# RWKV stage of a hybrid decoder step: ScalarE without transfers, one root per group-norm row, the chain's y through a dead tile, later pooling and key transposition

## The chip, the core and the metric

The kernel runs on one core of a Trainium2 chip. TensorE (PE in the profile) does the matrix products, VectorE (DVE) and ScalarE (ACT) the work on rows, GpSimd (POOL) some small copies, and SyncE (SP) issues most of the transfers (DMA). Each engine executes its own instructions strictly in their order and waits at an instruction until the semaphores that it names have come. The metric is the device time of one execution in microseconds.

## The reference, cut to what matters

One layer of a decoder trunk, over 1024 prompt tokens and 8 requests of 8 tokens each, 1088 columns in all; D_MODEL is 1024, with 8 heads of 64.

```python
P = h @ w_in                       # h: RMSNorm and adaLN of x
pr, pp, pg = jnp.split(P, ...)     # RWKV columns, pooling columns, gates
o_r = rwkv7_branch(pr)             # state S per head, updated token by token:
#   sa = -S kk;  S = S * w + sa (kk a)^T + v k^T;  y = S r
#   y = (y - mean(y)) * rsqrt(var(y) + GN_EPS) * ln_w + ln_b   per head
#   y = (y + bonus) * g,  g = sigmoid(xg) @ g2
o_p = pool_branch(pp)              # means over 2/4/8/16 tokens, minus the token, @ pool_w
merged = sigmoid(g_r) * (o_r @ w_br_rwkv) + sigmoid(g_p) * (o_p @ w_br_pool)
x = x + gt * (merged @ w_out)
x = x + gt2 * (square(relu(h2 @ w_ff1)) @ w_ff2)
y = rms_norm(x, norm_final)
```

The outputs are y, the new token-shift and pooling buffers and the new RWKV states, for the prompt and for the requests.

## The kernel before

Features lie on the 128 partitions and tokens along the row, so a row is 128 x 1088. Each big product is done three times in a one-pass format, with weights and inputs cut into a rounded half (hi) and the rest (lo): hi hi, hi lo, lo hi. A row is cut into the column blocks CH of 364, 362 and 362. A job is one output block of 128 features: it loads its weights (`weights`, L391: a transfer on SP, hi on ScalarE, lo on VectorE or, for every second one from the 68th on, on POOL), multiplies over all input blocks into three PSUM banks named mm, and evicts them.

The first stage (`phase1`, L1401) interleaves two streams on TensorE. The **background** is a list of jobs: 14 for the RWKV columns (`rwkv_cols`), four for pooling (`pool_cols`), each followed by two gate jobs, then eight more gate jobs (`gate`), then eight branch jobs for the pooling branch (`op_job`, L1474). The second gate job of a pooling group is held until that group's pooling is done. The row tiles px (two of them) and d are shared in turn by all of these; an `op_job` loads its gate row th into one of them when it begins, uses it in the eviction at its end, and stores it from there. The **foreground** is a set of generators: `heads`, `chains`, `pools` and `or_rows`. One head row f (0 to 3) holds two heads. For each, `front` makes the decay, keys and queries; `scores` runs `unit` three times (prompt half 0, the samples, prompt half 1); `inverse`, `level` and `affine` invert the triangular system of every 64-token block and turn it into block-wise state updates; `sample` does the requests; `post` is group norm, bonus and output gate. `chain` carries the state S from block to block, 8 steps in each half, and gives y in a PSUM bank named wc. `post` of row f - 1 runs beside `inverse`, `level` and `affine` of row f; for the last row it comes at the end, in pieces (`piece`). After this stage the second stage (`phase2`) starts with jobs that multiply all four rows of `post`.

**What sets the order.** TensorE's order is written out by a planner in the program (`Pace.run`, L272): it keeps a time, adds an estimate for each product, and asks the foreground generators in their order whether their next step is due; if none is, it emits one background step of three products. A step says when it is due by `need` (L378): the planner's estimate of when its operands are ready plus `spare` (300 ns by default), and of when the PSUM banks it takes are free (`Need.at`, L220). `Clocks` (L79) keeps these estimates, with a cost for each instruction. The planner decides the order alone; on the chip TensorE then waits where an operand is late. The other engines' orders and the slots of the tiles are chosen by the framework's scheduler from a simulation, not by the program. Foreground products use the PSUM banks named w (two), and for the chain wc (two).

The places that the change touches:

- `pools` (L774): per group and column block, `need(z, plw, zs, wait=0)` and a product with `pool_w`.
- `unit` (L909): after the decays are multiplied into the tile bk, values and r/a rows are transposed on TensorE (evicted to uv by ScalarE, to at by VectorE), then the keys bk four blocks at a time (`tr`, the products at L389), evicted to ab.
- `chain` (L1119): y of each half leaves its bank in two copies of 256 columns on ScalarE, through one buffer of its own, each stored by SP; the state goes out at the end.
- `sample` (L1161): loads the requests' state s0 into one of three hv tiles and stores the new one from it.
- `post` (L1217): five tiles named wt are shared by all rows of this part. `rinv` (L561) is a root on ScalarE and a reciprocal on VectorE, per column block. `gate` loads g2, then bv (the bonus), then sg (sigmoid of xg), multiplies g2 with sg and leaves the product in sg. `self.wt(over)` tells the planner which tile's place the new one is thought to take.

Of the kernel before, what the change touches and what calls it, by code (L numbers as in the profile page):

```python
# [9 lines left out]
F32 = mybir.dt.float32  # L10
# [8 lines left out]
P = 128  # L19
# [59 lines left out]
class Clocks:  # L79
# [5 lines left out]
    def __init__(self, pace):  # L85
        self.pace, self.on = pace, False
        self.busy = {"vector": [], "scalar": [], "gpsimd": [], "sync": []}
        self.seen, self.slots, self.table = {}, {}, 0
# [125 lines left out]
class Need:  # L214


    def __init__(self, k, aps, banks, wait, spare):
        self.k, self.aps, self.banks, self.wait, self.spare = k, aps, banks, wait, spare

    def at(self):  # L220
        return max([self.k.clocks.ready(*self.aps) + self.spare] + [self.k.clocks.free(b, self.k.pb[b], self.banks.count(b)) for b in set(self.banks)])

    def __call__(self):
        return self.at() <= self.k.pace.t
# [97 lines left out]
class K:  # L322
# [52 lines left out]
    def room(self, ns=1000, eng="vector"):  # L375
        return Room(self, eng, ns)

    def need(self, *aps, banks=("w",), wait=1000, spare=300):  # L378
        return Need(self, aps, banks, wait, spare)

    def tr(self, out, in_, ident):
        if self.mode != (P, P):
# [178 lines left out]
    def rinv(self, ps, n, out, scale, eps):  # L561
        nc = self.nc
        nc.scalar.activation(out, ps[:, :n], AF.Sqrt, bias=self.eps[:, eps:eps + 1], scale=scale)
        for a in range(0, n, 182):
            nc.vector.reciprocal(out[:, a:min(a + 182, n)], out[:, a:min(a + 182, n)])

# [141 lines left out]
    def gate(self, b, dst):  # L708
        nc = self.nc
        S = {}  # L710

        def begin():
            th = S["th"] = self.px()
            return lambda c0, n, ps: nc.scalar.activation(th[:, c0:c0 + n], ps[:, :n], AF.Tanh, scale=0.5)

        return Job(self.w_in(b), begin, after=lambda: nc.sync.dma_start(dst, S["th"][:, :NT]), xs=self.hx_rows)
# [57 lines left out]
    def pools(self):  # L774

        nc = self.nc
        self.pl = {}
        for g in range(4):
            plw = self.pxp.tile([P, P], F32, tag="plw", bufs=1, name=self.nm("plw"))
            nc.sync.dma_start(plw, self.io["pool_w"][:, g * 128:(g + 1) * 128])  # L780
            yield lambda: ("pool", g) in self.done
            z, zs, hi, lo = self.pl[g]
            for c0, n in CH:
                m = min(n, NPR - c0)
                yield self.need(z[:, c0:c0 + m], plw, zs, wait=0)
                ps = self.ps("w")
                self.mm(ps[:, :m], plw, z[:, c0:c0 + m], start=True, stop=True)
                if m < n:
                    self.mm(ps[:, m:n], plw, zs, start=True, stop=True)
                sc = self.par("pool_scale", g)  # L790
                nc.scalar.activation(hi[:, c0:c0 + n], ps[:, :n], AF.Copy, scale=sc)
                nc.vector.scalar_tensor_tensor(lo[:, c0:c0 + n], ps[:, :n], sc, hi[:, c0:c0 + n].bitcast(F32), op0=ALU.mult, op1=ALU.subtract)
            nc.sync.dma_start(self.d_op[0][g], hi.bitcast(F32))
            nc.sync.dma_start(self.d_op[1][g], lo.bitcast(F32))
            self.done.add(("op", g))
# [113 lines left out]
    def unit(self, f, d, u):  # L909
# [66 lines left out]
            nc.vector.tensor_copy(at[:, :, 0, :], cut(pa))  # L976
        for a in range(0, C, 4):
            m = min(4, C - a)
            yield self.need(bh[:, a:a + m], wait=0)
            ps = self.ps("w")  # L980
            for i in range(m):
                self.tr(ps[:, i * 128:(i + 1) * 128], bh[:, a + i, :], ident)
            nc.scalar.activation(ab[:, a:a + m, :, 64:128], ps[:, :m * 128].rearrange("p (c h j) -> p c h j", h=2, j=64), AF.Copy)
# [135 lines left out]
    def chain(self, f, d):  # L1119

        nc = self.nc
        end = d["end"]
        S = None
        for u in range(2):
            yield lambda: ("s", f, u) in self.done
            Q = d["qs"][u]
            uv, ab, ra = Q["uv"], Q["ab"], Q["ra"]
            yield self.need(uv, ab, ra, banks=("wc", "wc"))
            pn, py = self.ps("wc"), self.ps("wc")
            for ps, w, x in ((pn, ab[:, :, :, 64:128], uv), (py, uv, ab[:, :, :, 0:64])):  # L1130
                for i in range(8):
                    for h, hs in enumerate(HB):
                        self.mm(ps[hs, i * 64:(i + 1) * 64], w[:, i, h, :], x[:, i, h, :], start=i == 0, stop=False, skip_group_check=True)
            for i in range(8):
                c = 8 * u + i
                at = slice(i * 64, (i + 1) * 64)
                S1 = self.sm.tile([P, 64], F32, tag="S", bufs=3, name=self.nm("S"))
                if S is None:
                    nc.vector.tensor_copy(S1, pn[:, at])
                else:  # L1140
                    for hs in HB:
                        self.mm(pn[hs, at], ra[hs, i, 1, :], S[hs, :], start=False, stop=True, skip_group_check=True)
                    nc.vector.scalar_tensor_tensor(S1, S, end[:, c:c + 1], pn[:, at], op0=ALU.mult, op1=ALU.add)
                    for hs in HB:
                        self.mm(py[hs, at], S[hs, :], ra[hs, i, 0, :], start=False, stop=True, skip_group_check=True)
                S = S1
                if i < 7:
                    yield self.need(S, banks=(), wait=LS[f], spare=700)
            us = slice(u * 512, (u + 1) * 512)
            if f == 3:  # L1150
                nc.scalar.activation(self.y3[:, us], py, AF.Copy)
            else:
                for a in (0, 256):
                    y = self.sm.tile([P, 256], F32, tag="y", bufs=1, name=self.nm("y"))
                    nc.scalar.activation(y, py[:, a:a + 256], AF.Copy)
                    nc.sync.dma_start(self.d_y[f][:, us][:, a:a + 256], y)
            self.done.add(("c", f, u))
        nc.scalar.dma_start(self.io["o_wp"][f], S)
        self.done.add(("c", f))

    def sample(self, f, d):  # L1161
# [3 lines left out]
        qv = lambda t: t.rearrange("p (q v) -> p q v", v=64)  # L1165
        iv = self.hv
        s0 = iv()
        nc.scalar.dma_start(s0, self.io["s0"][f])
        qm = self.kc("qm")
        um = iv()  # L1170
        x, x2 = (sm.tile([P, 64], F32, tag="xs", bufs=2, name=self.nm("x")) for _ in range(2))
# [40 lines left out]
            self.mm(pn[hs, :], ab[:, 0, h, 64:128], ums[h], start=True, stop=True)  # L1212
        nc.vector.tensor_tensor(qv(s0), qv(s0), end[:, 16:24].unsqueeze(2).to_broadcast([P, 8, 64]), op=ALU.mult)
        nc.vector.tensor_tensor(s0, s0, pn, op=ALU.add)
        nc.scalar.dma_start(self.io["o_ws"][f], s0)

    def post(self, f):  # L1217

# [5 lines left out]
        else:  # L1224
            y = self.wt()
            nc.sync.dma_start(y, self.d_y[f])
        sq = self.wt()

        def gate(*over):
            g2 = self.sm.tile([P, P], F32, tag="sw", bufs=2, name=self.nm("sw"))  # L1230
            nc.sync.dma_start(g2, self.io["g2"][:, fs])
            bv, sg = self.wt(*over[:1]), self.wt(*over[1:])
            nc.sync.dma_start(bv, self.d_bv[f])
            nc.sync.dma_start(sg, self.d_x[13])
            for c0, n in CH:
                yield self.need(g2, sg[:, c0:c0 + n], wait=0)
                ps = self.ps("w")
                self.mm(ps[:, :n], g2, sg[:, c0:c0 + n], start=True, stop=True)
                nc.scalar.activation(sg[:, c0:c0 + n], ps[:, :n], AF.Copy)
            return bv, sg  # L1240

        if last:
            bv, sg = yield from gate()

        def piece(c0, n):
            s = slice(c0, c0 + n)
# [26 lines left out]
        else:  # L1273
# [10 lines left out]
            for c0, n in CH:  # L1284
                s = slice(c0, c0 + n)
                yield self.need(hi[:, s], lo[:, s], wait=0)
                self.rinv(self.sums(hi[:, s], lo[:, s]), n, sq[:, s], 1.0 / 64, 2)
                nc.vector.tensor_tensor(y[:, s], y[:, s], sq[:, s], op=ALU.mult)
                nc.scalar.activation(y[:, s], y[:, s], AF.Identity, bias=self.par("ln_b", f), scale=self.par("ln_w", f))
            yield self.need(y[:, 0:1], banks=(), wait=0)  # L1290
# [2 lines left out]
            nc.vector.tensor_tensor(y, y, sg, op=ALU.mult)  # L1293
            hi, lo = (self.row(self.p1, "wt", 5, F32R) for _ in range(2))
            self.halves(y, hi, lo)
            nc.sync.dma_start(self.d_or[0][f], hi.bitcast(F32))
            nc.sync.dma_start(self.d_or[1][f], lo.bitcast(F32))
        self.done.add(("or", f))
# [175 lines left out]
    def op_job(self, m):  # L1474
        nc = self.nc
        S = {}

        def begin():
            th = S["th"] = self.px() if m % 3 < 2 else self.row(self.pxp, "d", 1, w=PXW)
            nc.scalar.dma_start(th[:, :NT], self.d_th[8 + m])  # L1480
            return lambda c0, n, ps: nc.vector.scalar_tensor_tensor(th[:, c0:c0 + n], th[:, c0:c0 + n], 1.0, ps[:, :n], op0=ALU.add, op1=ALU.mult)

        return Job([self.io["w_br"][m][:, 512:1024]], begin, after=lambda: nc.sync.dma_start(self.d_th[8 + m], S["th"][:, :NT]), xs=lambda: self.op)
# [670 lines left out]
```

## Time and profile before

| | |
|---|---|
| median of 3 runs | 1640.77 us (1637.1 to 1644.98) |
| the profiled execution's own time | 1639.04 us |
| its span, first to last instruction | 1637.1 us |
| busy: PE, DVE, ACT, POOL | 1555.8, 1092.3, 681.1, 131.9 us |
| mean clock of TensorE | 0.989 |

How to read the lines: `PE w L358 <- ACT wt` means that TensorE stood idle before a product into a bank w, and that ScalarE's instruction that wrote wt ended last; the figures are total, times and longest. L358 is the helper that issues all products, L389 the one that issues transposes, L187 the helper through which all other engines' instructions go, so tiles tell more than lines. In a timeline line come the start, the time, engine and operation, the tile written and the tiles read, and in brackets the idle time of that engine before it and what ended it. In a line of stretches come the stretch and its length, the busy time of PE, its weight loads, DVE, ACT and POOL with their instructions, then the granted clock, the share of the transfers and GB/s. DMA engines' queues are SPq, ACTq and POOLq after the engine that issues.

### The profile page before, as it was taken

How to read it: one execution, taken by the hardware profiler on the slowest of the kernel's cores; microseconds unless marked ns; L12 is line 12 of the kernel's file. 1: busy time of each engine (PE TensorE's matmuls, PEld its weight loads, DVE VectorE, ACT ScalarE, POOL GpSimd, SP SyncE). 2: the span in 40 equal slices, each digit the busy share in tenths (PEclk: the TensorE clock that was granted, in tenths of full speed). 3: DMA queues.
4: the chain of work that ended last, by engine and by line, in shares of the span. 5: the costliest groups of instructions: out<-in, count | busy, mean ns of one | idle time of the engine just before them, and what ended most of it. 6: DMA issues, size and time to landing. Idle time of an engine off the chain costs nothing.

```text
span 1637.1 us, 34576 instructions
## 1 busy us (share of the span) xinstructions
PE 1555.8 (95%) x14107; PEld 1463.0 (89%) x14107; DVE 1092.3 (67%) x1916; ACT 681.1 (42%) x1313; POOL 131.9 (8%) x200
## 2 busy tenths in 40 slices
PE   4999999899898989989999999999999999999997
PEld 2898888798797878978989999999999999999997
DVE  4585575765757475836643678899766886566775
ACT  4454364355233553533322465222333434434651
POOL 0110000000000000000520120000000041000000
PEclk9999999999999989999999999999999999999999
DMA  9233513233313312664786455766444996664663
GB/s 344 93 105 103 194 58 103 71 115 131 106 58 122 131 64 88 246 229 151 248 329 234 155 179 180 235 217 217 151 148 152 399 352 232 212 200 152 214 203 122
DMA packets 121855, 288.25 MB, mean 176 GB/s; under 512 B 21120, under 2 KB 26752, under 8 KB 121696
## 3 DMA queue, kind: packets, MB, share of 16 engines
q1 hardware_dynamic: 113312, 264.65, 46.7%
q10 hardware_dynamic: 8240, 20.95, 3.8%
q8 instruction: 111, 1.82, 0.4%
q0 software_dynamic: 144, 0.44, 0.1%
q14 instruction: 48, 0.39, 0.1%
HBM read 208.70 MB, written 77.28 MB: 175 GB/s over the span
## 4 chain that ended last, share of the span: by engine, by line
PE 59%; DMA 5%; DVE 4%; ACT 2%; issue 1%; POOL 1%; SPq 0%; DVEq 0%; ACTq 0%; POOLq 0%
PE mm L358 39%; PE wc L358 12%; PE w L358 8%; DMA wt<-d_x 1%; DMA mg<-in_w_ff 1%; DMA hid<-in_w_ff 1%; DMA hx<-d_oph 1%; POOL t L187 1%; DVE hx L187 1%; DVE hv L187 1%; DMA wraw<-in_w_br 1%; DVE wlo L187 1%; DMA t<-d_th 0%; DVE bk L187 0%; DVE px L187 0%
## 5 line engine op out<-in xcount | busy, mean ns | idle before, releaser
L358 PE MATMUL mm<-hx,whi 128*128 128x362 f32 (+2 forms) x2944 | 690.7, 322 | 10.7 <-ACT px L187 9.3
L358 PEld LDWEIGHTS mm<-hx,whi 128*128 128x128 f32 x2944 | 499.0, 190 | 34.3 <-issue 12.0
L358 PE MATMUL mm<-hx,wlo 128*128 128x362 f32 (+2 forms) x1472 | 463.6, 315 | 2.1 <-DVE wlo L187 2.1
L358 PEld LDWEIGHTS mm<-hx,wlo 128*128 128x128 f32 x1472 | 279.5, 190 | 2.6 <-DVE wlo L187 2.6
L358 PE MATMUL mm<-mg,whi 128*128 128x272 f32 (+2 forms) x1312 | 249.3, 289 | 0.0
L358 PEld LDWEIGHTS mm<-mg,whi 128*128 128x128 f32 x1312 | 205.3, 188 | 4.2 <-issue 2.5
L358 PE MATMUL mm<-mg,wlo 128*128 128x272 f32 (+2 forms) x656 | 188.5, 287 | 0.0
L358 PE MATMUL wc<-hx,whi 128*128 128x272 f32 x896 | 170.3, 287 | 0.0
L358 PEld LDWEIGHTS wc<-hx,whi 128*128 128x128 f32 x896 | 140.3, 188 | 0.0
L187 ACT ACTIVATE whi<-hid 128x512 fp32r<-128x512 f32 x128 | 80.4, 629 | 143.7 <-PE mm L358 59.1
L358 PE MATMUL wc<-hx,wlo 128*128 128x272 f32 x448 | 128.8, 287 | 0.7 <-DVE wlo L187 0.7
L358 PEld LDWEIGHTS mm<-mg,wlo 128*128 128x128 f32 x656 | 123.5, 188 | 0.0
L187 DVE TENSOR_TENSOR wlo<-hid,whi 128x512 fp32r<-128x512 f32 x128 | 88.0, 688 | 48.7 <-ACT whi L187 47.6
L187 DVE TENSOR_TENSOR wlo<-wraw,whi 128x512 fp32r<-128x512 f32 x84 | 60.9, 726 | 81.2 <-ACT whi L187 81.1
L187 ACT ACTIVATE whi<-wraw 128x512 fp32r<-128x512 f32 x100 | 62.8, 628 | 86.7 <-PE mm L358 43.7
L358 PE MATMUL w<-hx,whi 128*128 128x272 f32 (+1 forms) x480 | 96.9, 296 | 0.0
L358 PEld LDWEIGHTS wc<-hx,wlo 128*128 128x128 f32 x448 | 84.2, 188 | 0.9 <-DVE wlo L187 0.9
L187 POOL TENSOR_TENSOR hx<-hx,rs 128x64 f32<-128x64 f32 x24 | 35.2, 1466 | 569.3 <-DMA mg<-in_w_ff 361.5
L358 PEld LDWEIGHTS mm<-mg,hx 128*128 128x128 f32 x576 | 72.9, 188 | 5.0 <-issue 5.0
L358 PEld LDWEIGHTS w<-hx,whi 128*128 128x128 f32 x480 | 77.0, 188 | 0.0
L358 PE MATMUL mm<-mg,hx 128*128 128x272 f32 (+2 forms) x576 | 75.5, 290 | 0.0
L358 PE MATMUL w<-hx,wlo 128*128 128x272 f32 (+1 forms) x240 | 70.8, 295 | 0.8 <-DVE wlo L187 0.8
(269 smaller groups left out, 2308.7 us busy)
## 6 DMA issues: line engine op xcount, KB each, us to landing
t<-d_t SPq DMA_DIRECT2D x56, 544.0 KB, 4.8
hid<-in_w_ff SPq DMA_DIRECT2D x110, 256.0 KB, 3.8
d_t<-hx SPq DMA_DIRECT2D x102, 272.0 KB, 2.2
hid<-in_w_ff SPq DMA_DIRECT2D x42, 512.0 KB, 3.7
wraw<-in_w_in SPq DMA_DIRECT2D x68, 256.0 KB, 2.8
mg<-in_w_ff SPq DMA_DIRECT2D x58, 256.0 KB, 5.4
hid<-in_w_ada_mlp SPq DMA_DIRECT2D x24, 512.0 KB, 5.7
d_th<-px SPq DMA_DIRECT2D x22, 544.0 KB, 3.0
```

The source lines that it names most:

```text
L187: return f(*a, **kw)
L358: return self.nc.tensor.matmul(out, lhsT, rhs, **kw)
```

## The change

- The transfers of the RWKV stage that ScalarE issued (the state o_wp of a chain, s0 and o_ws of the requests, the gate row of each `op_job`) are issued by POOL.
- In `post` of the first three rows a new `inv` makes var + eps (Identity on ScalarE) and its reciprocal per column block, and one root over the whole row follows; the products with it come after. `front` and the last row's pieces keep `rinv`.
- `chain` evicts y in one copy of 512 columns into the first part of its unit's tile at, which isn't read any more by then, and stores it in one transfer.
- `gate` takes and loads sg before bv; in the last row it takes the places of tiles that the third row's `post` leaves, and sq is taken after it.
- `Need` gets a `slack` that is added to the time when banks come free. The keys' transposition is due at `spare=900, slack=600`, pooling at `spare=6000`.

```diff
-        return max([self.k.clocks.ready(*self.aps) + self.spare] + [self.k.clocks.free(b, self.k.pb[b], self.banks.count(b)) for b in set(self.banks)])
+        return max([self.k.clocks.ready(*self.aps) + self.spare] + [self.k.clocks.free(b, self.k.pb[b], self.banks.count(b)) + self.slack for b in set(self.banks)])
...
+    def inv(self, ps, n, out, scale, eps):
+        nc = self.nc
+        nc.scalar.activation(out, ps[:, :n], AF.Identity, bias=self.eps[:, eps:eps + 1], scale=scale)
+        for a in range(0, n, 182):
+            nc.vector.reciprocal(out[:, a:min(a + 182, n)], out[:, a:min(a + 182, n)])
...
-                yield self.need(z[:, c0:c0 + m], plw, zs, wait=0)
+                yield self.need(z[:, c0:c0 + m], plw, zs, wait=0, spare=6000)
...
-            yield self.need(bh[:, a:a + m], wait=0)
+            yield self.need(bh[:, a:a + m], wait=0, spare=900, slack=600)
...
-                for a in (0, 256):
-                    y = self.sm.tile([P, 256], F32, tag="y", bufs=1, name=self.nm("y"))
-                    nc.scalar.activation(y, py[:, a:a + 256], AF.Copy)
-                    nc.sync.dma_start(self.d_y[f][:, us][:, a:a + 256], y)
+                y = Q["at"].rearrange("p c s j -> p (c s j)")[:, 0:512]
+                nc.scalar.activation(y, py, AF.Copy)
+                nc.sync.dma_start(self.d_y[f][:, us], y)
...
-        nc.scalar.dma_start(self.io["o_wp"][f], S)
+        nc.gpsimd.dma_start(self.io["o_wp"][f], S)
...
-        nc.scalar.dma_start(s0, self.io["s0"][f])
+        nc.gpsimd.dma_start(s0, self.io["s0"][f])
...
-        nc.scalar.dma_start(self.io["o_ws"][f], s0)
+        nc.gpsimd.dma_start(self.io["o_ws"][f], s0)
...
-        sq = self.wt()
...
-            bv, sg = self.wt(*over[:1]), self.wt(*over[1:])
+            sg, bv = (self.wt(x) for x in over)
+            nc.sync.dma_start(sg, self.d_x[13])
             nc.sync.dma_start(bv, self.d_bv[f])
-            nc.sync.dma_start(sg, self.d_x[13])
...
-            bv, sg = yield from gate()
+            bv, sg = yield from gate(*self.held[:2])
+            sq = self.wt(self.held[2])
+        else:
+            sq = self.wt()
...
-                self.rinv(self.sums(hi[:, s], lo[:, s]), n, sq[:, s], 1.0 / 64, 2)
+                self.inv(self.sums(hi[:, s], lo[:, s]), n, sq[:, s], 1.0 / 64, 2)
+            nc.scalar.activation(sq, sq, AF.Sqrt)
+            for c0, n in CH:
+                s = slice(c0, c0 + n)
                 nc.vector.tensor_tensor(y[:, s], y[:, s], sq[:, s], op=ALU.mult)
...
+            self.held = sg, y, hi
...
-            nc.scalar.dma_start(th[:, :NT], self.d_th[8 + m])
+            nc.gpsimd.dma_start(th[:, :NT], self.d_th[8 + m])
```

More of the change, by code (lines that the diff above doesn't have):

```diff
@@ L214, with __init__ @@
 class Need:
-    def __init__(self, k, aps, banks, wait, spare):
-        self.k, self.aps, self.banks, self.wait, self.spare = k, aps, banks, wait, spare
+    def __init__(self, k, aps, banks, wait, spare, slack):
+        self.k, self.aps, self.banks, self.wait, self.spare, self.slack = k, aps, banks, wait, spare, slack
     def at(self):
-        return max([self.k.clocks.ready(*self.aps) + self.spare] + [self.k.clocks.free(b, self.k.pb[b], self.banks.count(b)) for b in set(self.banks)])
+        return max([self.k.clocks.ready(*self.aps) + self.spare] + [self.k.clocks.free(b, self.k.pb[b], self.banks.count(b)) + self.slack for b in set(self.banks)])
     def __call__(self):
@@ L376, in room, with need @@
         return Room(self, eng, ns)
-    def need(self, *aps, banks=("w",), wait=1000, spare=300):
-        return Need(self, aps, banks, wait, spare)
+    def need(self, *aps, banks=("w",), wait=1000, spare=300, slack=0):
+        return Need(self, aps, banks, wait, spare, slack)
     def tr(self, out, in_, ident):
```

## The prediction

> **What bounds the kernel now.** I read the page first, then the busy time by stages, then TensorE's waits in the stage that the change touches, then the engine behind each wait.
>
> ```profile
> PE 1555.8 (95%) x14107; PEld 1463.0 (89%) x14107; DVE 1092.3 (67%) x1916; ACT 681.1 (42%) x1313; POOL 131.9 (8%) x200
> 160.00:440.00 280.00, 260.49 (x3017) 231.20 (x3014) 186.77 (x341) 126.28 (x255) 17.49 (x49) 0.98 0.34 110
> 440.00:715.00 275.00, 248.51 (x2837) 225.35 (x2836) 167.76 (x313) 125.59 (x257) 7.71 (x18) 0.97 0.37 130
> 715.00:785.00 70.00, 70.00 (x705) 61.91 (x704) 40.78 (x78) 21.43 (x43) 5.85 (x6) 1.00 0.49 171
> 785.00:1637.00 852.00, 840.50 (x6616) 826.28 (x6615) 599.58 (x1036) 326.46 (x609) 84.37 (x68) 1.00 0.63 216
> ```
>
> TensorE is the bound, and the change alters none of its work. What can be won is time in which it stands still. In the RWKV stage that is 19.5 us (280 less 260.49) and 26.5 us (275 less 248.51): 46 us, all of it before 715. After 785 the stage is another and the change doesn't touch it. TensorE's waits between 160 and 830, as total, times and longest:
>
> ```profile
> PE mm L358 <- ACT px L187: 9.3, 5, 3.5
> PE w L358 <- DVE tt L187: 5.5, 1, 5.5
> PE w L358 <- DVE hv L187: 5.2, 2, 5.1
> PE w L358 <- DMA wt<-d_x: 4.4, 1, 4.4
> PE w L389 <- DVE at L187: 3.9, 4, 1.6
> PE wc L358 <- ACT y L187: 3.0, 1, 3.0
> PE w L389 <- ACT uv L187: 2.4, 3, 1.5
> ```
>
> A long wait costs twice, since the clock then runs at half speed for a while. These are the stretches at half clock that follow the long waits above (length, TensorE busy, further on the clock):
>
> ```profile
> 305.90:312.70 6.80, 5.83 (x15) 4.47 (x16) 5.59 (x22) 1.13 (x2) 0.00 (x0) 0.50 0.00 1
> 415.10:418.50 3.40, 3.34 (x62) 3.34 (x64) 2.58 (x4) 0.52 (x2) 0.00 (x0) 0.50 0.11 39
> 432.20:435.60 3.40, 3.40 (x14) 3.40 (x12) 3.40 (x7) 0.00 (x0) 0.26 (x1) 0.50 0.49 119
> 497.00:500.40 3.40, 3.18 (x8) 2.41 (x8) 2.69 (x12) 0.56 (x1) 0.00 (x0) 0.51 0.02 5
> 701.80:705.30 3.50, 3.50 (x10) 2.96 (x11) 1.09 (x2) 1.32 (x3) 0.00 (x0) 0.51 0.38 100
> ```
>
> Half of the busy time is lost in each: 2.9, 1.7, 1.7, 1.6 and 1.7 us.
>
> **The change part by part.** The sum is made against the profiled execution's own 1639.04 us (span 1637.1). The median of the runs is 1640.77, so 1.7 us are added at the end.
>
> *Pooling 6 us later.* The waits named tt and hv (5.5 and 5.1) are the first pooling products of two groups; the names are those of the VectorE instruction that ended last. Six microseconds of background put before them would cover both. With the half clock (2.9 and 1.6) that is 15.1 us at most. The other end is 0: the products only change places with gate products, so no loss of work. I take 8, about half, because VectorE is nearly full around these waits, so that the next product that needs it may wait instead:
>
> ```profile
> 500.00:520.00 20.00, 18.43 (x187) 17.22 (x186) 17.80 (x34) 8.46 (x16) 1.32 (x5) 0.99 0.37 133
> ```
>
> By the code the second gate job of a group is held until its pooling is through, so there is one gate job of cover and no more.
>
> *Key transposition later.* The waits at L389 are 3.9 and 2.4 us, seven of the 20 groups (four heads, two groups for each prompt unit, one for the sample unit). They end with at or uv, the evictions that free the PSUM banks, so of the two numbers it is the slack of 0.6 us that helps: at most 7 x 0.6 = 4.2. The loss: 13 groups that didn't wait come up to 0.9 us later, and that lies on the heads' chain (slower rival below). I take a gain of 3.
>
> *ScalarE issues no transfers.* Of the stage's transfers s0, o_ws, o_wp and the gate rows of the branch jobs go to POOL's queue. ScalarE executes in order, and three times it stood still at such an issue:
>
> ```profile
> 429.58 0.63 ACT L187 ACTIVATE whi<-wraw 128x512 fp32r<-128x512 f32 x1 [3.96 <-DVE S L187]
> 690.57 0.47 ACT L187 ACTIVATE px<-mm 128x362 f32<-128x362 f32 x1 [3.38 <-DMA hx<-d_opl]
> 709.36 0.59 ACT L187 ACTIVATE hv<-w 32x512 f32<-32x512 f32 x1 [4.82 <-DMA d_th<-px]
> 430.62 0.60 PE L358 MATMUL mm<-hx,whi 128*128 128x362 f32 x2 [3.54 <-ACT px L187]
> 691.10 0.60 PE L358 MATMUL mm<-hx,whi 128*128 128x362 f32 x2 [1.18 <-ACT px L187]
> 710.61 0.88 PE L358 MATMUL w<-wt,sw 128*128 128x362 f32 x2 [0.96 <-ACT hv L187]
> ```
>
> TensorE waited 3.54 + 1.18 + 0.96 = 5.7 us right behind them, with the half clock at 432 7.4. The 4.82 also held the copies of the head's own chain (hv), so that chain gains as well. I take 6; the ends are 7.4 and a loss of as much, if POOL's other work were needed as soon. On POOL the issue itself is short, and the queue has room (131.9 us busy):
>
> ```profile
> 1.98 0.54 POOL L187 DMA_DIRECT2D kct<-in_kc  x1
> kct<-in_kc POOLq DMA_DIRECT2D x1, 314.5 KB, 7.2
> px<-d_th ACTq DMA_DIRECT2D x6, 544.0 KB, 4.5
> ```
>
> Behind a waiting transfer stand POOL's copies of the shift rows (they hand px back), its z blocks and every second lo half of a weight; the weights are two jobs ahead, the gate rows are first needed when their job ends. So a row that lands 2.7 us later (7.2 against 4.5) costs nothing as long as that lead lasts; were it gone, 2.7 for each of eight jobs.
>
> [...]
>
> *The chain's y.* Two copies through one buffer, the second behind the first's transfer:
>
> ```profile
> 414.72 0.38 ACT L187 ACTIVATE y<-wc 128x256 f32<-128x256 f32 x1 [1.80 <-DMA d_y<-y]
> ```
>
> TensorE waited 3.0 us for the bank that this copy frees, and 1.7 at half clock. One copy into the dead tile needs no transfer first. The tile at is then held until its transfer has landed, but the next unit writes it only after that head's front. Ends 4.7 and 0; I take 4.
>
> *One root per row.* For three of the four heads three roots become three identities, the reciprocals stay, and one root follows. What falls away are reloads of ScalarE's table:
>
> ```profile
> 541.05 1.28 ACT L187 ACT_TABLE_LOAD   x1
> 542.87 0.60 PE L358 MATMUL mm<-hx,whi 128*128 128x362 f32 x2 [3.20 <-ACT px L187]
> ```
>
> An eviction stood behind that load, and TensorE waited 3.20 us. But the one root is longer and waits for all reciprocals in front of the next eviction, so 3.2 is one end and minus 2.6 (two loads in one piece) the other. I take a gain of 1.5.
>
> *The gate's rows first.* For the third head bv was loaded at 677.87 and sg, which the first product needs, only at 691.58:
>
> ```profile
> 677.87 0.46 SPq L187 DMA_DIRECT2D wt<-d_bv  x1
> 691.58 0.32 SPq L187 DMA_DIRECT2D wt<-d_x  x1
> ```
>
> With sg in the first place the 4.4 us and the 1.7 at half clock go, since bv is used only after the products. Ends 6.1 and 0; I take 5.5.
>
> Together 8 + 3 + 6 + 4 + 1.5 + 5.5 = 28. **What comes back:** the order of the whole stage is planned anew, and the three ScalarE stalls (3.96, 3.38, 4.82) become POOL stalls. I set two new waits of about 2.5 us with 1.7 us of half clock each against it: 8. That leaves 20: 1639.0 - 20 + 1.7 = **1621 us**.
>
> **The rivals.**
>
> *Waits only move (20%).* VectorE sets the pace where pooling and keys wait (17.80 of 20 us), so those waits return one product later, and the POOL queue gives back what ScalarE gains. Left are the gate's 5.5 and y's 4, less about 6 for new waits: 1637. For it speaks that L389 itself waits for VectorE's at; against it that three of the waits end with ScalarE or a transfer.
>
> *All of it comes out (12%).* The upper ends, 15.1 + 4.2 + 7.4 + 4.7 + 3.2 + 6.1 = 40.7, with nothing back: 1600. Against it: every replanned order has had waits.
>
> *The heads' chain sets the end (10%), slower.* Background work that fills a wait is missing at the end of the stage. The last product of the heads, the eviction that ends their row and the branch work around it:
>
> ```profile
> 772.32 0.77 PE L358 MATMUL w<-wt,kct 128*128 128x362 f32 x2
> 779.88 0.49 PE L358 MATMUL w<-hx,whi 128*128 128x362 f32 x2
> 780.37 0.49 PE L358 MATMUL mm<-hx,whi 128*128 128x364 f32 x2
> 781.63 0.51 ACT L187 ACTIVATE hx<-wt 128x362 fp32r<-128x362 f32 x1 [2.03 <-DVE wt L187]
> ```
>
> At 779.88 the first job that needs all heads is at the last column block of the first of its four weights; the next block begins 0.49 us later, three blocks to a weight. So the same block of the fourth weight, which reads this head's last columns, comes 9 x 0.49 = 4.4 us on, at 784.3. Those columns are there at 782.1 (781.63 + 0.51) and VectorE's lo half behind it, about as long again, 782.7. Some 1.6 us are to spare. If the later keys stretch the chain by 20 x 0.9 = 18 us, and the gate's 5.5 is all that the chain gains, the end moves by 18 - 1.6 - 5.5 = 11 us: 1639 + 11 + 1.7 = 1652. It decides as soon as the stretch is over what the chain itself gains plus 1.6. Against it: the waits for sg and for hv lie on the chain and shorten it.
>
> *POOL's transfers come late (6%).* [...]
>
> **How the numbers follow.** The forecast has 52%, with a range of its own from 1610 to 1633. A measurement of this kernel tells 0.5% (8.2 us) from no change: faster is below 1632.6, slower over 1649. Faster: nearly all of the 52, the 12, a quarter of the 20 and a little of the 6, together 67%. Slower: most of the 10 and a tail, 10%. Same: 23%. The range of 8 in 10 runs from 1601, which leaves out half of the case where all comes out, to 1645, which leaves out the slower rival.
>
> **What would show it.** Right: no wait of TensorE for y, for wt<-d_x or at pooling over 1 us; no ScalarE idle ended by a transfer before 785; two table loads in each group norm of the first three heads; fewer than three of the five quoted stretches at half clock. Wrong: waits of the same sum named DVE at, S or hv (waits only moved); TensorE idle between 740 and 800 (the chain); POOL's lo halves or wt late in TensorE's waits (POOL). A new long wait in the first 300 us would show that the planning, not an edit, decided.

## The result, and the profile after

| | before | after |
|---|---|---|
| median of 6 runs each, same chip | 1643.2 us (1637.1 to 1652.09) | 1607.57 us (1599.9 to 1608.58) |
| ratio after to before | | 0.9775, 95% interval [0.9754, 0.9797] |
| profiled execution, its span | 1639.04, 1637.1 us | 1607.54, 1605.8 us |

The change makes the kernel 36 us faster by the medians, 31.5 us between the two profiled executions. Forecast were 1621 and a gain of 20.

The first two fences are of the changed kernel: the page's busy times, and its stretches (PE, weight loads, DVE, ACT, POOL, then granted clock). The stage now ends before 753, so the limits of the last two stretches differ from those shown of before.

```profile
PE 1548.2 (96%) x14107; PEld 1459.7 (91%) x14107; DVE 1088.1 (68%) x1916; ACT 664.7 (41%) x1296; POOL 136.8 (9%) x220
```

```profile
160.00:440.00 280.00, 269.26 (x3179) 240.73 (x3178) 194.44 (x360) 127.31 (x268) 19.05 (x54) 0.99 0.35 118
440.00:715.00 275.00, 265.25 (x3207) 241.23 (x3206) 173.91 (x332) 117.20 (x249) 16.66 (x34) 0.98 0.43 150
715.00:753.00 38.00, 38.00 (x233) 34.68 (x234) 25.69 (x45) 12.21 (x22) 5.20 (x6) 1.00 0.43 145
```

In the first two, TensorE stands still for 10.7 and 9.8 us, where it was 19.5 and 26.5, and does 160 and 370 more products in the same time. The stage is best compared whole. It ends where the first product of the first job that needs all heads begins its last column block; that was 779.88, and is now:

```profile
744.12 0.49 PE L358 MATMUL w<-hx,whi 128*128 128x362 f32 x2
```

The stretch from 90 to that end, first of the kernel before, then of the changed one:

```profile
90.00:779.88 689.88, 643.88 (x7088) 577.76 (x7086) 444.68 (x812) 309.78 (x637) 37.66 (x94) 0.98 0.36 121
```

```profile
90.00:744.12 654.12, 633.63 (x7093) 572.81 (x7092) 440.74 (x812) 293.55 (x620) 44.15 (x114) 0.99 0.37 128
```

The same number of products (five records more). The stage is 35.8 us shorter: idle time falls from 46.0 to 20.5 (25.5), and the same products are busy for 10.3 us less, mostly because fewer of them run at half clock. Behind the stage there were 857.2 us (1637.1 - 779.88); there are now 861.7 (1605.8 - 744.12). So 4.5 us are given back there. They lie at one load, which is issued 37.6 us after the end of the stage (781.74 less 744.12) where it was 35.4 (815.28 less 779.88). TensorE waits for it twice, 3.0 us in total, and runs at half clock around these waits (the last stretch of the fence of such stretches below). The longer wait:

```profile
792.23 1.92 PE L358 MATMUL wc<-hid,sT 128*32 128x512 f32 x4 [2.30 <-DMA hid<-in_w_ada_mlp]
```

What is left of TensorE's waits between 160 and 785 in the changed kernel (total, times, longest):

```profile
PE wc L358 <- DVE S L187: 5.9, 6, 1.9
PE mm L358 <- ACT px L187: 3.6, 1, 3.6
PE w L358 <- DVE px L187: 3.0, 3, 1.8
PE w L358 <- issue: 2.9, 2, 2.0
PE w L358 <- ACT wt L187: 1.6, 3, 1.2
PE w L358 <- ACT iv L187: 1.3, 1, 1.3
PE mm L358 <- DVE px L187: 0.8, 1, 0.8
PE w L358 <- ACT z L187: 0.7, 1, 0.7
PE w L389 <- DVE at L187: 0.5, 2, 0.3
```

The waits named y, tt, hv and wt<-d_x are gone, L389 falls from 6.3 to 0.5, ScalarE's px from 9.3 to 3.6, its wt from 4.4 to 1.6. Waits came back too. The chain's state S grew most; VectorE's px at a product into w grew from 0.6 to 3.0 and issue (idle time for which the profile shows no wait) from 1.1 to 2.9, and iv, z and VectorE's px at mm are new. Lines that shrank lost 35.1 us, lines that grew gained 9.7. Of before, S was

```profile
PE wc L358 <- DVE S L187: 3.2, 2, 1.8
```

The stretches at half clock from 90 us on in the changed kernel, all but the last inside the stage:

```profile
409.70:413.10 3.40, 3.40 (x13) 3.40 (x12) 2.65 (x4) 0.00 (x0) 0.56 (x1) 0.50 0.20 77
542.80:546.20 3.40, 3.40 (x25) 3.00 (x27) 1.65 (x3) 1.58 (x4) 0.00 (x0) 0.50 0.30 91
573.50:576.90 3.40, 3.33 (x16) 2.51 (x18) 3.39 (x6) 1.87 (x4) 0.61 (x2) 0.50 0.94 347
658.90:662.30 3.40, 3.40 (x13) 3.40 (x13) 0.61 (x2) 2.35 (x4) 1.13 (x1) 0.50 1.04 413
791.75:798.58 6.83, 5.64 (x14) 2.30 (x15) 1.16 (x3) 0.00 (x0) 2.46 (x1) 0.52 1.03 408
```

Four of 3.4 us are 13.6 us in the stage, where the trace of before has 30.7 us: the five stretches that the prediction quotes and a sixth, the longest,

```profile
589.20:599.40 10.20, 8.47 (x24) 6.50 (x24) 8.47 (x14) 6.75 (x11) 0.00 (x0) 0.50 0.43 136
```

TensorE is busy in 27.7 us of the 30.7 and in 13.5 of the 13.6. By the granted clock of 0.50 half of the difference, 7.1 us, is lost time that is no longer lost. That is an estimate: in the changed kernel three products of a job take 0.91 us from 658.65 to 659.56, in the last of its four stretches, and 0.49 from 662.28 to 662.77, just behind it, which makes it 6.5 us. Either figure accounts for most of the 10.3.

### The profile page after: what moved, and what is told of

It is laid out like the page before. It is cut to its first block, busy times and chain, and to the rows that moved or that the text cites. A ratio compares the mean times of both kernels' runs of the same rounds, so it can differ in the third digit from the quotient of the medians.

```text
span 1605.8 us, 34570 instructions
## 1 busy us (share of the span) xinstructions
PE 1548.2 (96%) x14107; PEld 1459.7 (91%) x14107; DVE 1088.1 (68%) x1916; ACT 664.7 (41%) x1296; POOL 136.8 (9%) x220
## 4 chain that ended last, share of the span: by engine, by line
PE 73%; DVE 6%; DMA 4%; issue 2%; ACT 1%; POOL 0%; SPq 0%; DVEq 0%; ACTq 0%; POOLq 0%
PE mm L358 49%; PE wc L358 13%; PE w L358 11%; DVE wt L187 2%; DMA mg<-in_w_ff 1%; DMA hx<-d_oph 1%; DMA hid<-in_w_ada_mlp 1%; DVE hv L187 1%; DVE wlo L187 1%; DMA wt<-d_x 1%; DVE bk L187 1%; DMA d_th<-px 1%; DVE hx L187 0%; POOL t L187 0%; PE w L389 0%
## 5 line engine op out<-in xcount | busy, mean ns | idle before, releaser
L187 ACT ACTIVATE px<-mm 128x362 f32<-128x362 f32 (+3 forms) x113 | 46.2, 435 | 70.5 <-PE mm L358 66.2
```

The costliest lines, as they stand in the source:

```text
L187: return f(*a, **kw)
```

## The experiments

The planner recomputes TensorE's whole order whenever its estimates alter. So each edit can act in two ways: by its own instructions, and by the order that comes with it. Three groups of runs tell these apart. Below, "against after" is the median less 1607.57, and "same" means that the program holds TensorE's products in the order of the changed kernel, each at its place; the other engines' orders are then nearly the same too. The runs of the table were made on other occasions than the result, beside runs of before with medians from 1640.16 to 1643.38 us. By the ratios to before, no_dma costs 10 us, no_gate 4, root_same_order 1, y_same_order 6 and three_same_order 14, so that the last column is good to some 4 us.

| run | what differs from the changed kernel | TensorE's order | median us (range) | ratio to before [95%] | against after |
|---|---|---|---|---|---|
| no_dma | transfers on ScalarE | same | 1614.09 (1610.14 to 1616.7) | 0.9838 [0.9809, 0.9868] | +6.5 |
| no_gate | bv before sg, tiles as before | same | 1608.77 (1602.28 to 1615.71) | 0.9801 [0.9763, 0.9840] | +1.2 |
| root_same_order | root per block | same | 1606.94 (1603.66 to 1612.02) | 0.9781 [0.9758, 0.9804] | -0.6 |
| y_same_order | y in two copies | same | 1612.43 (1606.72 to 1617.11) | 0.9809 [0.9784, 0.9833] | +4.9 |
| three_same_order | transfers, root and y as before | same | 1620.15 (1616.21 to 1622.01) | 0.9858 [0.9834, 0.9881] | +12.6 |
| no_root | root per block | new | 1625.95 (1622.4 to 1626.21) | 0.9894 [0.9866, 0.9921] | +18.4 |
| no_y | y in two copies | new | 1614.37 (1611.89 to 1617.22) | 0.9835 [0.9808, 0.9863] | +6.8 |
| no_pool | pooling's spare 300 | new | 1619.77 (1618.51 to 1621.75) | 0.9869 [0.9844, 0.9893] | +12.2 |
| no_keys | keys' spare 300, slack 0 | new | 1617.76 (1617.38 to 1618.95) | 0.9844 [0.9822, 0.9867] | +10.2 |
| table_1283 | one number of the planner | new | 1625.73 (1624.14 to 1629.11) | 0.9895 [0.9877, 0.9914] | +18.2 |
| more_slack | longer spares, pooling and S | new | 1648.56 (1643.57 to 1656.58) | 1.0045 [1.0024, 1.0067] | +41.0 |
| keys_far | longer spare and slack, keys | new | 1656.63 (1654.22 to 1659.8) | 1.0081 [1.0054, 1.0107] | +49.1 |

**One edit undone at a time.** Six runs put one edit back; in two of them the order stays the same, in four it doesn't.

```diff
# no_pool
-                yield self.need(z[:, c0:c0 + m], plw, zs, wait=0, spare=6000)
+                yield self.need(z[:, c0:c0 + m], plw, zs, wait=0)
```

> The changed kernel (1607.6 us) with pooling due as before the change. Theory of own waits: each edit takes the waits that stood at its own place and leaves the others; pooling's two long waits and their half-clock stretches come back, 8 to 15 us, so 1616 to 1623. Rival, planning: the order of the whole stage is laid out anew by any edit, so what an edit is worth has little to do with the waits at its place; then 1600 to 1630 with no relation to 8 to 15, and the waits of TensorE that grow are others than those before pooling's products.

```diff
# no_dma (and s0, o_ws and the op_job's gate row likewise)
-        nc.gpsimd.dma_start(self.io["o_wp"][f], S)
+        nc.scalar.dma_start(self.io["o_wp"][f], S)
```

> The changed kernel with the 20 transfers back on ScalarE's queue. Own waits: 6 to 7.4 us slower, 1613.6 to 1615, with ScalarE idle before instructions behind an issue and TensorE waiting for px or hv there. Planning: no relation. A third reading, that POOL's issue costs something and hides part of the gain: faster than 1607.6.

```diff
# no_y
-                y = Q["at"].rearrange("p c s j -> p (c s j)")[:, 0:512]
-                nc.scalar.activation(y, py, AF.Copy)
-                nc.sync.dma_start(self.d_y[f][:, us], y)
+                for a in (0, 256):
+                    y = self.sm.tile([P, 256], F32, tag="y", bufs=1, name=self.nm("y"))
+                    nc.scalar.activation(y, py[:, a:a + 256], AF.Copy)
+                    nc.sync.dma_start(self.d_y[f][:, us][:, a:a + 256], y)
```

> The changed kernel with y in two copies through one buffer. Own waits: 4 to 4.7 us slower, 1611.6 to 1612.3, and TensorE waits for wc behind ScalarE's y. Planning: the planner counts the buffer's wait too and lays the second half of each chain later, so that more than 4.7 comes back: over 1615, with the heads' later products later by as much.

```diff
# no_gate (and sq taken first, no tiles held)
-            sg, bv = (self.wt(x) for x in over)
-            nc.sync.dma_start(sg, self.d_x[13])
+            bv, sg = self.wt(*over[:1]), self.wt(*over[1:])
             nc.sync.dma_start(bv, self.d_bv[f])
+            nc.sync.dma_start(sg, self.d_x[13])
```

> The changed kernel with bv loaded before sg and the tiles of the last row taken as before. Own waits: 5.5 to 6.1 us slower, 1613 to 1613.7, with TensorE's wait for wt<-d_x back near the end of the stage. Planning: no relation, and no such wait.

no_dma shows the stall coming back as it was read before. ScalarE stands at an issue whose tile is still being stored, and the copies behind it come late; the fence holds ScalarE's and TensorE's lines of that run:

```profile
678.47 1.19 ACT L187 ACTIVATE z<-w 32x512 f32<-32x512 f32 x2 [5.54 <-DMA d_th<-px]
679.71 0.88 PE L358 MATMUL w<-wt,sw 128*128 128x362 f32 x2 [2.13 <-ACT z L187]
```

In the changed kernel POOL stands before two such loads, for 6.20 and 3.61 us (the profile puts the first down to a load of weights), and no wait of TensorE follows either:

```profile
673.22 0.53 POOL L187 DMA_DIRECT2D px<-d_th  x1 [6.20 <-DMA wraw<-in_w_br]
677.36 0.54 POOL L187 DMA_DIRECT2D px<-d_th  x1 [3.61 <-DMA d_th<-px]
```

```profile
px<-d_th POOLq DMA_DIRECT2D x6, 544.0 KB, 4.4
```

The last line is of the view of DMA issues: these six rows land 4.4 us after their issue, where they took 4.5 from ScalarE's queue. (The two rows of the tile d took 5.7 against 4.6, the requests' states 3.8 against 2.8.) So the 6.5 us are this edit's own price, with the order unchanged.

no_y brings back the wait for the bank, 3.34 us:

```profile
406.25 1.98 PE L358 MATMUL wc<-uv,ab 128*64 128x64 f32 x32 [3.34 <-ACT y L187]
```

no_gate costs nothing that can be told: sg is loaded second again, and still no product waits for it, because in this order the first of the gate's products comes 18.5 us behind the load. In the kernel before it began 10.2 us behind it (691.58 to 701.8), after its wait of 4.4:

```profile
655.25 0.32 SPq L187 DMA_DIRECT2D wt<-d_x  x1
673.80 1.41 PE L358 MATMUL w<-wt,sw 128*128 128x364 f32 x2
```

Pooling due as before (no_pool) falls into the range of the own waits, but its trace doesn't give back the two long waits of before: VectorE's px and hv at a product into w are 6.1 and 2.1 us, the longest 3.8, where the changed kernel has 3.0 for px and 1.3 for iv; and S is 9.2 where it is 5.9. The other two, keys and root, cost far more than the waits they were meant for.

```diff
# no_keys
-            yield self.need(bh[:, a:a + m], wait=0, spare=900, slack=600)
+            yield self.need(bh[:, a:a + m], wait=0)
# no_root
-                self.inv(self.sums(hi[:, s], lo[:, s]), n, sq[:, s], 1.0 / 64, 2)
-            nc.scalar.activation(sq, sq, AF.Sqrt)
-            for c0, n in CH:
-                s = slice(c0, c0 + n)
+                self.rinv(self.sums(hi[:, s], lo[:, s]), n, sq[:, s], 1.0 / 64, 2)
```

> The changed kernel with the keys' transposition due as before. Own waits: 3 to 4.2 us slower, 1610.6 to 1611.8, with waits before the products at L389 of about 6 us in total again. Planning: no relation, and other waits grow.

> The changed kernel with a root per column block as before. Own waits: 1.5 to 3.2 us slower, 1609 to 1610.8, with eight more table loads or so. If instead the one root is what keeps TensorE from waiting for sg (it lays the gate's products later, so that the load has time, which would explain why undoing the gate's order alone cost only 1.2 us): 5 us and more slower. If the six edits add up, the two runs of this call together are 36 - 26.7 = 9 us slower.

In no_keys only part of the wait at L389 comes back, 2.7 and 1.4 us. In no_root most of what is lost lies at one place. The group norm's sums and a pooling group wait in a row, 13.4 us, and the clock stays at half for 23.9 us, in which TensorE is busy for 12.40 and so loses 6.2 more (an estimate by the clock of 0.50); TensorE's lines, then VectorE's, then the stretch:

```profile
492.36 0.59 PE L358 MATMUL w<-wt,bones 128*128 128x362 f32 x2 [1.78 <-ACT wt L187]
494.54 0.67 PE L358 MATMUL w<-wt,bones 128*128 128x362 f32 x1 [1.58 <-ACT wt L187]
498.46 0.67 PE L358 MATMUL w<-wt,bones 128*128 128x362 f32 x1 [3.26 <-DVE wt L187]
505.87 2.79 PE L358 MATMUL w<-px,plw 128*128 128x364 f32 x4 [6.73 <-DVE px L187]
```

```profile
492.70 2.43 DVE L187 RECIPROCAL wt<-wt 128x182 f32<-128x182 f32 x2
495.53 2.41 DVE L187 RECIPROCAL wt<-wt 128x182 f32<-128x182 f32 x2
...
503.41 2.37 DVE L187 RECIPROCAL wt<-wt 128x182 f32<-128x182 f32 x2
```

```profile
493.90:517.80 23.90, 12.40 (x31) 9.23 (x32) 15.43 (x22) 7.74 (x14) 1.31 (x5) 0.50 0.27 103
```

The reciprocals, 2.4 us for a column block, stand on VectorE between the chain that makes the pooling rows and the group norm. no_keys meets the same crowd:

```profile
495.53 0.67 PE L358 MATMUL w<-wt,bones 128*128 128x362 f32 x1 [5.23 <-DVE wt L187]
```

In the changed kernel the pooling products are through before 489, and the reciprocals follow at 500.26 in one piece, in front of the single root, where nothing waits for them:

```profile
500.26 7.01 DVE L187 RECIPROCAL wt<-wt 128x182 f32<-128x182 f32 x6 [0.76 <-ACT wt L187]
```

Is it the root that keeps them apart, or the order that was laid with it? The next group answers that.

**Old instructions, new order.** Here the planner is shown the instructions of the changed kernel, while others are issued. TensorE's list of products stays the same, so that what is lost is the instructions' own.

```diff
# root_same_order; three_same_order does so for y too and has ScalarE's transfers
-                self.inv(self.sums(hi[:, s], lo[:, s]), n, sq[:, s], 1.0 / 64, 2)
-            nc.scalar.activation(sq, sq, AF.Sqrt)
+                ps = self.sums(hi[:, s], lo[:, s])
+                self.planned(lambda: self.inv(ps, n, sq[:, s], 1.0 / 64, 2))      # planner only
+                self.unplanned(lambda: self.rinv(ps, n, sq[:, s], 1.0 / 64, 2))   # issued only
+                self.unplanned(lambda: scaled(s))
+            self.planned(lambda: nc.scalar.activation(sq, sq, AF.Sqrt))
```

> The changed kernel, but the three roots per group norm (with the products behind them) are issued as before, while the planner is told of the single root, so that TensorE's order is that of the changed kernel, product for product. Theory A (own work): the root's 18.4 us, which the time lost when it alone was undone with a new order, are its instructions; then 1624 to 1627 here. Theory B (order): the instructions cost about five more table loads of 1.28 us, of which one or two stand in front of an eviction that TensorE waits for, 1 to 4 us; then 1608 to 1612, and the other 14 or so belong to the order that the planner laid with the longer estimate, in which the group norm of the third head met pooling and the inversion on VectorE.

> The changed kernel, but y leaves its bank in two copies through one buffer, as before, in the changed kernel's order on TensorE, product for product. Theory A (own work): the 6.8 us lost when it alone was undone, 1614. Theory B (order): the wait of 3.0 us for the bank and 1.7 us at half clock that the profile of before shows, 4.7 at most and none where the next use of the bank lies far off: 1608 to 1612.

> ScalarE's transfers, the roots per block and y's two copies all as before, in the changed kernel's order on TensorE. Theory A (own work): 6.5 + 18.4 + 6.8 = 31.7 us lost, 1639, so that nearly nothing of the gain is left. Theory B (order): the transfers' 6.5 (there the order was the same already), 1 to 4 for the roots and 1 to 4.7 for y: 1616 to 1623; more than half of the gain stays with the order alone. If the stalls meet on ScalarE it may be some us more than the sum.

The root's instructions are worth nothing that can be told: 1606.94, and a stage with the idle time of the changed kernel, 20.4 us (655.67 less 635.26).

```profile
90.00:745.67 655.67, 635.26 (x7088) 572.04 (x7087) 439.36 (x810) 291.64 (x617) 44.41 (x114) 0.99 0.37 127
```

So the 18.4 us of no_root are the order's. Even the table loads that fell away are mostly the order's: between 160 and 715 there are 24 before, 11 after, and with the roots per block in the new order 12. The groups of table loads (count, busy us, mean ns, then idle time before them) of before, after and root_same_order:

```profile
L187 ACT ACT_TABLE_LOAD x24 | 30.8, 1283 | 1.0 <-PE mm L358 0.5
```

```profile
L187 ACT ACT_TABLE_LOAD x11 | 14.1, 1283 | 9.1 <-DVE wt L187 7.2 <-PE w L358 1.7
```

```profile
L187 ACT ACT_TABLE_LOAD x12 | 15.4, 1283 | 1.9 <-PE w L358 1.7
```

y's two copies cost 4.9 us in this order; its interval overlaps that of the changed kernel, but its trace has the wait back:

```profile
PE wc L358 <- ACT y L187: 4.2, 3, 1.9
```

The three together cost 12.6, close to 6.5 - 0.6 + 4.9 = 10.8. In three_same_order, ScalarE's stall holds up the gate's product for longer than in no_dma:

```profile
686.00 1.57 PE L358 MATMUL w<-wt,sw 128*128 128x362 f32 x2 [4.76 <-ACT z L187]
```

So with the old transfers, roots and copies, the new order (with the gate's rows first) still runs at 1620.15, 23 us under the 1643.2 of before. What these instructions add is 12.6.

**New order, nothing else.** The last question is how much an order may differ by chance. One number of the planner is altered, by 17 ns; every instruction stays. With TensorE's order, those of VectorE and ScalarE change too, so that "the order" means the whole plan.

```diff
# table_1283
-                    ns, self.table = ns + 1300, tb
+                    ns, self.table = ns + 1283, tb
```

> The changed kernel with one number of the planner altered: a reload of ScalarE's table is priced 1283 ns, as the traces measure it, and not 1300. No instruction is other, but the planner lays another order from the middle of the second head on. Theory A (each edit has its own price, and the planner adds little): 1606 to 1609, as the changed kernel. Theory B (any new order draws new waits): off by more than 3 us, to either side, and rather slower (1610 to 1625), since the changed kernel's order has few waits left.

It costs 18.2 us, half of the whole gain. The stage's stretch, and two of its waits:

```profile
90.00:765.19 675.19, 646.51 (x7092) 581.39 (x7091) 441.67 (x810) 292.60 (x620) 45.21 (x114) 0.97 0.36 124
```

```profile
PE wc L358 <- DVE S L187: 11.4, 8, 2.6
PE mm L358 <- DVE px L187: 6.2, 2, 4.8
```

Idle time is 28.7 us and not 20.5, and the products are busy for 646.5 us and not 633.6, at a clock of 0.97. Waits and half clock share the loss. This is one such order; how far others lie apart isn't shown.

**Longer spares.** If later products were better as such, more of it would help, or do no harm.

```diff
# keys_far
-            yield self.need(bh[:, a:a + m], wait=0, spare=900, slack=600)
+            yield self.need(bh[:, a:a + m], wait=0, spare=4000, slack=4000)
# more_slack
-                yield self.need(z[:, c0:c0 + m], plw, zs, wait=0, spare=6000)
+                yield self.need(z[:, c0:c0 + m], plw, zs, wait=0, spare=6000, slack=1500)
-                    yield self.need(S, banks=(), wait=LS[f], spare=700)
+                    yield self.need(S, banks=(), wait=LS[f], spare=1500)
```

> The changed kernel with the keys' transposition due 4000 after operands and banks instead of 900 and 600. Chain theory (the forecast's slower rival: the heads' chain can set the end of the stage): 20 groups by some 3.4 us lay the chain up to 68 us later; background runs out before the heads are through, TensorE stands idle at the end of the stage by that less the 8 us of cover, 1630 to 1667. Own waits without such an end: the keys wait no more at all and the background fills, 1605 to 1612.

> The changed kernel with 1500 more on the banks of pooling's products and the chain's steps due 1500 after S instead of 700; these are the two largest waits left (S 5.9 us, pooling's px 3.0). Own waits: up to 8 us faster, 1600 to 1605. Chain theory: the chain of states gets longer by 56 steps of 0.8 us but runs beside the heads, so only the last row's could reach the end: 1600 to 1612. Planning: anything between 1597 and 1620, with waits of other names.

Both are slower than the kernel before, by 0.8 and 0.45 per cent, and lose more than twice what table_1283 loses. Whether that is more than an unlucky order isn't shown by one neutral order. No theory foresaw more_slack: S fell from 5.9 to 4.8 us as meant, but the waits at L389 grew from 0.5 to 6.8 and VectorE's px at a product into w from 3.0 to 6.3. In keys_far a pooling group waited longest of all waits in the stage, in any of these traces; the second line is the end of its stage:

```profile
445.59 2.79 PE L358 MATMUL w<-px,plw 128*128 128x364 f32 x4 [12.63 <-DVE px L187]
715.00:789.40 74.40, 65.83 (x876) 54.23 (x875) 39.22 (x71) 27.86 (x53) 7.30 (x10) 0.91 0.39 132
```

The chain theory, whose range held the time, explains the smaller part. At the end the background is used up (its last product begins at 769.92) and TensorE waits at the last pieces of the group norm, but it stands idle for 8.6 us behind 715 and for 45.8 us before.

## Why the prediction was right, and where it was wrong

**The bound and the direction: right.** TensorE's idle time in the stage and the half clock behind it were all that could be won, and all of the gain is there: 25.5 and 10.3 us of 35.8.

**The size: short by 13 to 16 us** (the time by 13, the gain by 16). The forecast's own range, 1610 to 1633, missed 1607.57; only the range with the rivals holds it. Two steps of the sum failed.

- *What the order brings:* pooling 8 and keys 3 act by the order alone, and 8 were set against them for what comes back, so the order was put at 3 us. By the runs it is worth some 22: 1643.2 less 1620.15 is 23, and 1.2 of that is the gate's (by the ratios it is 19). Waits did come back, 9.7 us of them, with three of the four stretches at half clock at new places. But more went away than the terms took: ScalarE's wt and uv at products into w, 4.2 us together, and the sixth stretch at half clock, in which 4.2 us were lost by the same kind of estimate; no term counted either. Another 4.5 us came back behind the stage.
- *Terms by edit:* the sum gave each edit the wait that it was aimed at. By its own instructions the root was worth -0.6 and not 1.5, the gate's rows 1.2 and not 5.5; the transfers 6.5 against 6 and y 4.9 against 4 were well sized. The four were put at 17 together and measured some 14 (12.6 for the three, 1.2 for the gate; by the ratios 18). Undone one at a time, the six edits lose 12.2 + 6.5 + 6.8 + 1.2 + 10.2 + 18.4 = 55.3 us, more than the 36 there are, so they can't each have a price of that kind.

So the direction was right for a reason that the forecast had only in part: it looked for nearly all of the gain in the edits' own work, and by these figures half of it or more came with the order.

**Pooling 8 and keys 3** can't be priced. They are nothing but order, and no_pool's 12.2 and no_keys' 10.2 lie within the 18.2 that a neutral order cost. What the runs do show is that the waits they were aimed at went: at pooling 10.7 us became at most 4.3 (3.0 under the name px, 1.3 under iv), at L389 6.3 became 0.5. How much of the order's share comes from these two rules, and how much is the luck of this one order, stays open; table_1283 has both rules and all new instructions, and gains 18 of the 36.

**The rivals.** Waits only move (1637): no, 9.7 us came back for 35.1 that went. All of it comes out (1600): nearer than the forecast, but not for its reason, since waits did come back, and of the four terms measured by themselves only y's reached its upper end (4.9 against 4.7). The heads' chain sets the end (1652): TensorE is busy for all 38.00 us from 715 to 753, so not here; keys_far at 1656.63 looks like that rival by its time, but 45.8 of its 54.4 us of idle time lie before 715. POOL's transfers late (6%): no. That chance was the author's estimate; what was to hold the transfers up isn't shown. No wait of TensorE followed POOL's two stalls above, 6.20 and 3.61 us. The issues of the stage took 0.53 to 0.57 us each, and by the landings above the rows of px came no later (4.4 us against 4.5), those of d and the requests' states about 1 us later (5.7 against 4.6, 3.8 against 2.8).

**The signs named beforehand.** No wait for y or wt<-d_x: right. No pooling wait over 1 us: wrong, 1.78 at 487.70 and 1.26 at 430.09 are left. Two table loads in each group norm: right for two rows, with one at the root (334.14, 507.35) and one behind it (365.67, 512.23); the third row has only that at 661.41. No ScalarE idle that a transfer ends: wrong. None is at a transfer that ScalarE issues, but three in the stage are at loads that SP issues, and behind one of these stands TensorE's longest wait left in the stage:

```profile
540.20 1.39 ACT L187 ACTIVATE wt<-wt,part 128x512 f32<-128x512 f32 x2 [3.65 <-DMA wt<-d_x]
542.78 0.97 PE L358 MATMUL mm<-hx,whi 128*128 128x362 f32 x2 [3.61 <-ACT px L187]
```

ScalarE took its work in order here: the activation for the heads that waited 3.65 us for its row held the eviction of px, which came at 542.27, behind it. Fewer than three of the five quoted stretches at half clock: right, one is left (at 415, now 410); the other three of the stage are at other places. The sign for a planning that decides, a new long wait in the first 300 us, did not come (the longest there is 1.9 us, for S), and the planning weighed most all the same: the sign looked for harm only.

## What to carry to other kernels

When a planner writes out the order, an edit's loss in a run that undoes it mixes its own price with a new order. Issue the old instructions under the plan of the new ones before crediting an edit, and alter one harmless number of the plan to get an idea how far orders differ by chance: here a single such order was 18 us slower, as much as any edit seemed to be worth. A wait whose cause is a crowd on another engine (here pooling, inversion and reciprocals on VectorE within 15 us) went away when the order spread the crowd, with the old root as with the new one.

## What was not expected of the hardware

In the traces of before and after the half clock comes in fixed windows, and the window before one need not be idle. The stretches last 3.4 us or a multiple, to 0.1, and in the trace of before the later five begin 32, 37, 56, 83 and 116 times 3.413 us behind the first, at 305.90; the 3.413 is worked out from these starts. In the 3.4 us just before the six stretches TensorE was busy for 0.00, 0.43, 1.58, 0.00, 1.42 and 0.02 us; in the changed kernel before its four in the stage for 1.66, 0.02, 2.73 and 1.42 us. The third of the six:

```profile
428.80:432.20 3.40, 1.58 (x15) 1.28 (x15) 3.40 (x5) 2.42 (x5) 1.20 (x2) 1.00 0.22 80
```

Where a wait fell seems to have counted, too. The wait of 3.20 us at 542.87 in the trace of before lay across two windows and left each half busy, and full speed went on:

```profile
537.96:541.37 3.41, 1.71 (x11) 1.41 (x9) 1.81 (x3) 3.36 (x5) 0.00 (x0) 1.00 0.54 163
541.37:544.78 3.41, 1.91 (x11) 1.91 (x12) 2.68 (x4) 2.56 (x5) 0.00 (x0) 1.00 0.08 32
```

No sharp limit can be read off: the changed kernel's window from 484.77 was busy for 1.63 us only, and full speed followed. And one stretch needed no long wait at all. At 573.50 in the changed kernel it follows 3.5 us in which TensorE was busy for 2.82, mostly in small products, with no wait over 0.53. What the clock's throttle counts there isn't shown:

```profile
570.00:573.50 3.50, 2.82 (x51) 1.91 (x49) 3.50 (x8) 2.15 (x5) 0.56 (x1) 1.00 0.53 156
```

The four runs of no_gate differ with the mean clock: they took 1602.28 us at 0.994, 1608.49 at 0.990, 1609.05 at 0.988 and 1615.71 at 0.987, from end to end about 1.9 us for each thousandth. How much of this a sum of waits would show isn't known, since each trace here is of one execution.
